# Two service rates of a side-work table in a hybrid attention/recurrence kernel on one core

## The chip, the cores and the metric

The kernel runs on one core of a Trainium2 chip. The metric is the device time of one execution in microseconds (us). The kernel before was timed three times: 4288.13, 4299.74 and 4304.53 us, median 4299.74 us. All rows of profiles below come from a further, profiled execution of 4318.05 us, whose span from the first to the last instruction was 4316.3 us.

## The reference

A latent of 1024 tokens and a context of 256 tokens (width 1024) run through two layers. Cut to what matters here:

```python
for l in range(DEPTH):                                   # DEPTH = 2
    h_lat = rmsnorm(xl, norm1_g[l]) * (1.0 + sc1) + sh1  # h_ctx likewise
    z_lat = jnp.split(h_lat @ w_in[l], IN_SPLITS, axis=-1)
    na_l, na_c = na_mixer(z_lat[0], z_ctx[0], ...)       # 2-D neighbourhood attention
    mla_l, mla_c = mla_mixer(z_lat[1], z_ctx[1], ...)    # latent attention
    rk_l, rk_c = rwkv7_mixer(z_lat[2], z_ctx[2], ...)    # bidirectional RWKV-7 recurrence
    df_l, df_c = diff_mixer(z_lat[3], z_ctx[3], ...)     # differential attention
    xl = xl + g1 * (concat([na_l, mla_l, rk_l, df_l]) @ w_out[l])
    xl = xl + g2 * conv_glu(rmsnorm(xl, ...) * (1.0 + sc2) + sh2, ...)
# the recurrence, both directions, over all tokens:
#   sa = S a_t ;  S = S * w_t + sa b_t^T + v_t k_t^T ;  y_t = S r_t
```

The recurrence is not stepped token by token. It is cut into chunks; inside a chunk the interactions become small triangular matrices, which are inverted once (32x32 blocks first, then joined to 64x64), so that the step over a chunk is a few matrix products.

## The kernel before, in words

**Staging of a layer.** The function `mix` (L1631) does the mixer of one layer in two stages. In the first, the generator `main` runs the input projection: for each group of weight columns, in the order recurrence, values, latent attention ("ml"), differential attention ("diff", written to `dfq` and `dfk`), neighbourhood attention ("na", written to `naq` and `nak`), it loads 512 KB of weights (`wst`), splits them on ACT and DVE into a rounded part `whi` and a rest `wlo` (L1219, L1220), and issues dense matmuls of `whi`, `wlo` on the two parts of the activations (L140, L141, L142, out `psd`), 24 to a chunk of tokens. Rotary work on DVE, ACT and POOL follows (L1332 to L1365) and writes to DRAM. In the second stage an attention loop runs over query blocks: scores `psL` from K and Q (L803), row maxima on DVE (L962, L964), exponentials on ACT (L973), transposes (L1011), products with V (L1032).

**Side work.** Beside both stages run generators that issue a piece of other work each time they are pulled. In the projection stage there are three: `prep_gen` (L283) prepares the recurrence in ten slots, eight or ten steps each (gram products `pg` on PE, L440; masks on DVE, L447 and L448; transposes `pbt`, L460; results to the DRAM buffers `rsg`, `rvt`, `rnt`). `lanes_gen` (L526) inverts the triangular blocks in three groups of slots (0 and 1; 2 to 5; 6 to 9). For each group it loads the blocks (`lM`), does 31 steps of one product and one reduction on DVE (L547, out `lpr`; L548, out `lXT`), copies (L552, `lX`), sends the results to DRAM and back (L554, L557, then L567, L569 and L570 into `G`), and joins blocks with 32x32 matmuls (`pmg`, L580 and L582; 64 of each for group one, 128 for the others). `mla_gen` projects the latent attention's compressed vectors (`mst`, `mpb`, `mpq`, `mpk`, `mpv`); it starts (L1687) once both the ml columns and the ten slots are done. In the attention stage the sides are `scan` (the recurrence proper; it loads `SG`, `VS`, `XB` and waits for the inverse of its slots), `ada` and `rwo`. A group that isn't finished when the projection ends is carried on in the attention stage.

**What sets the order.** `main` yields after every six dense matmuls, the attention loop after each piece of a block. After each yield `tick` pulls every side by its rate from a table:

```python
    s["acc"] += s["rate"]
    while s["acc"] >= 1 and s in self.sides:
        s["acc"] -= 1
        if not self.pull_hi(s["gen"], ...)
```

With rate 0.8 a side issues eight steps in ten ticks. The program order so made is not yet the order of the engines: the kernel is built with a scheduler (L2293) that orders each engine's instructions by this order as priority and by its own estimate of when inputs are ready. Each engine then runs its own list strictly in order, and SP issues almost all DMAs in one list.

Of the kernel before, what the change touches and what calls it, by code (L numbers as in the profile page):

```python
# [40 lines left out]
class K:  # L41
# [1707 lines left out]
    bf3 = (3, 4, 3)  # L1749
    lb2 = ((2, (4, 2, 1)),)  # L1750
    lb3 = ((3, (3, 2, 1)),)
    rates = dict(ada=0.2, prep=0.8, lanes=0.5, scan=0.8, mla=1.5, rwo=0.5)

    def wsp(self, o, n):
        a = max(0, min(n, SEQ - o))
# [545 lines left out]
```

## Time and profile before

| | us |
|---|---|
| median of three runs | 4299.74 |
| profiled execution | 4318.05 |
| its span | 4316.3 |
| PE busy (93% of the span) | 4027.8 |
| DVE busy (66%) | 2866.8 |
| ACT busy (46%) | 1982.7 |
| POOL busy (19%) | 801.9 |

The mean granted clock of TensorE was 0.955 of full speed. Busy time counts an engine's instructions, not what they achieve; a busy PE at half clock counts in full. In the trace the projection stage of the first layer lies between about 110 and 583 us, that of the second between about 2380 and 2846 us; at 583 and at 2846 us the attention stages begin. In the page's 40 slices (108 us each) the granted clock falls to 7 tenths in just two kinds of place besides the start: around these two beginnings.

### The profile page before, as it was taken

To read this page: it belongs to the slowest core of one execution; us is meant where nothing else is said; L and a number is where in the kernel's file an instruction comes from. 1 tells how busy PE (TensorE), PEld (TensorE's weight loads), DVE (VectorE), ACT (ScalarE), POOL (GpSimd) and SP (SyncE) were. 2 spreads that over 40 slices of the span, in tenths; PEclk is the share of its full clock that TensorE was granted. 3 is DMA by queue.
4 is the path that set the end of the run, shared out by engine and by line. 5 is a ranking of instruction groups with operands and counts; after the bars stand their busy time and mean duration, and the time that the engine had idled before them with its cause. 6 is when DMAs were issued, how large, how long until landed. Compare 5 with 4: busy or idle time off the path is not lost. (4 is left out here: it accounts for less than half of the span.)

```text
span 4316.3 us, 76712 instructions
## 1 busy us (share of the span) xinstructions
PE 4027.8 (93%) x29152; PEld 3319.9 (77%) x29152; DVE 2866.8 (66%) x5946; ACT 1982.7 (46%) x4386; POOL 801.9 (19%) x1320
## 2 busy tenths in 40 slices
PE   6999969999999999899998999969999999999998
PEld 4887856677777778788887887856677777788998
DVE  6577686656676765655556667686776766557666
ACT  4444435535554544433334444435545555435443
POOL 3244122212211112000001344122313111111000
PEclk7999979999999999999999999979999999999999
DMA  6444676655523243221213344687636332333332
GB/s 198 151 134 141 204 226 204 224 160 142 151 82 107 78 149 115 71 64 65 64 59 115 137 135 139 204 233 223 206 98 175 104 106 74 125 104 126 94 98 74
DMA packets 423199, 578.40 MB, mean 134 GB/s; under 512 B 109100, under 2 KB 287660, under 8 KB 421296
## 3 DMA queue, kind: packets, MB, share of 16 engines
q1 hardware_dynamic: 422832, 573.51, 42.9%
q8 instruction: 230, 3.77, 0.4%
q14 instruction: 137, 1.12, 0.1%
HBM read 433.47 MB, written 139.92 MB: 133 GB/s over the span
## 5 line engine op out<-in xcount | busy, mean ns | idle before, releaser
L141 PE MATMUL psm<-h_l,whi 128*128 128x512 f32 (+1 forms) x2112 | 710.3, 336 | 9.2 <-DVE h_l L258 9.0
L140 PE MATMUL psm<-h_h,whi 128*128 128x512 f32 (+1 forms) x2112 | 713.5, 338 | 2.3 <-ACT h_h L257 2.3
L142 PE MATMUL psm<-h_h,wlo 128*128 128x512 f32 (+1 forms) x2112 | 709.0, 336 | 0.0
L1888 DVE SCALAR_TENSOR_TENSOR x<-psm,mod,x 128x258 f32<-128x258 f32 (+2 forms) x616 | 327.0, 555 | 288.3 <-PE psm L142 287.9
L973 ACT ACTIVATE sm_P<-psL,sm_n 128x512 f32<-128x512 f32 (+1 forms) x672 | 392.8, 593 | 266.6 <-DVE sm_n L964 238.5
L141 PEld LDWEIGHTS psm<-h_l,whi 128*128 128x128 f32 x2112 | 399.4, 189 | 54.1 <-DVE h_l L258 12.0
L140 PEld LDWEIGHTS psm<-h_h,whi 128*128 128x128 f32 x2112 | 399.4, 189 | 52.0 <-DVE x L1888 4.0
L142 PEld LDWEIGHTS psm<-h_h,wlo 128*128 128x128 f32 x2112 | 399.1, 189 | 43.4 <-issue 0.2
L962 DVE TENSOR_REDUCE sm_m<-psL 128x1 f32<-128x512 f32 (+1 forms) x640 | 353.0, 578 | 88.0 <-PE psL L803 43.3
L140 PE MATMUL psm<-gh,dhi 128*128 128x510 f32 (+3 forms) x1056 | 364.8, 347 | 10.1 <-ACT mb L1852 5.1
L133 ACT ACTIVATE whi<-wst 128x1024 fp32r<-128x1024 f32 x176 | 186.6, 1060 | 401.2 <-PE psm L141 376.7
L141 PE MATMUL psm<-gl,dhi 128*128 128x510 f32 (+3 forms) x1056 | 357.7, 339 | 0.1
L142 PE MATMUL psm<-gh,dlo 128*128 128x510 f32 (+3 forms) x1056 | 357.4, 339 | 0.0
L134 DVE TENSOR_TENSOR wlo<-wst,whi 128x1024 fp32r<-128x1024 f32 x176 | 214.8, 1220 | 169.6 <-ACT whi L133 169.5
L1032 PE MATMUL psV<-PT,V 128*64 128x128 f32 x3488 | 299.3, 283 | 1.2 <-DVE sm_n L964 0.7
L1011 PE MATMUL psT<-ident,sm_P 128*128 128x128 f32 x1744 | 287.3, 287 | 10.6 <-DVE sm_P L1001 6.2
L1032 PEld LDWEIGHTS psV<-PT,V 128*64 128x64 f32 x3488 | 208.8, 137 | 83.7 <-issue 63.7
L1011 PEld LDWEIGHTS psT<-ident,sm_P 128*128 128x128 f32 x1744 | 206.4, 145 | 69.8 <-issue 29.7
L140 PEld LDWEIGHTS psm<-gh,dhi 128*128 128x128 f32 x1056 | 199.6, 189 | 44.6 <-ACT mb L1852 9.3
L142 PEld LDWEIGHTS psm<-gh,dlo 128*128 128x128 f32 x1056 | 200.2, 190 | 21.7
L141 PEld LDWEIGHTS psm<-gl,dhi 128*128 128x128 f32 x1056 | 200.4, 190 | 18.1 <-issue 0.7
L803 PE MATMUL psL<-K,Q 96*128 96x512 f32 (+1 forms) x400 | 148.8, 437 | 68.7 <-DMA Q<-dfq 34.4
(381 smaller groups left out, 9264.7 us busy)
## 6 DMA issues: line engine op xcount, KB each, us to landing
wst<-in_w_up_dram SPq DMA_DIRECT2D x176, 512.0 KB
wst<-in_w_down_dram SPq DMA_DIRECT2D x88, 512.0 KB
adw<-in_ada_w_dram SPq DMA_DIRECT2D x80, 512.0 KB
SG<-rsg SPq DMA_DIRECT2D x40, 896.0 KB
wst<-in_w_out_dram SPq DMA_DIRECT2D x96, 256.0 KB
rsg<-ARM SPq DMA_DIRECT2D x20, 1024.0 KB
K<-dfk SPq DMA_DIRECT2D x16, 960.0 KB
wst<-in_w_rw_dram SPq DMA_DIRECT2D x28, 512.0 KB
```

Source lines behind the costliest of these rows:

```text
L133: nc.scalar.activation(hi[:, :n], st[:, :n], AF.Copy)
L134: nc.vector.tensor_tensor(out=lo[:, :n], in0=st[:, :n], in1=hi[:, :n].bitcast(F32), op=ALU.subtract)
L140: mm(out, ah, bh, start=first, stop=False)
L141: mm(out, ah, bl, start=False, stop=False)
L142: mm(out, al, bh, start=False, stop=last)
L803: nc.tensor.matmul(ps, ld[0][0:96, j], ld[1][j // 2][0:96, j % 2, o:o + n], start=True, stop=True)
L962: nc.vector.tensor_reduce(out=m[:, j, i:i + 1], in_=src, axis=AX.X, op=ALU.max)
L973: ACT(Pt[:, off:off + n], s["L"][j][t][:, to:to + n], AF.Exp, bias=neg, accum_out=sm[:, j, i:i + 1])
L1011: nc.tensor.transpose(pt[:, j], Ph[:, (bb + j) * P:(bb + j + 1) * P], self.ident)
L1032: nc.tensor.matmul(s["po"][64 * h:64 * h + 64, 0], V[:, kts[i], h], s["PT"][h][:, i], start=i == 0, stop=i == nk - 1, tile_position=(0, 64 ...
L1888: STT(out=x[:, s:e], in0=ps[:, s:e], scalar=mod[:, v, 40 + m:41 + m], in1=x[:, s:e], op0=ALU.mult, op1=ALU.add)
```

## The change

One line of numbers (L1752). The preparation is pulled 1.3 times per six dense matmuls where it was 0.8, the inversion 1.2 times where it was 0.5. Nothing else differs; the instructions are the same but for 17 that PE has fewer of, of some 17,900 rows.

```diff
-    rates = dict(ada=0.2, prep=0.8, lanes=0.5, scan=0.8, mla=1.5, rwo=0.5)
+    rates = dict(ada=0.2, prep=1.3, lanes=1.2, scan=0.8, mla=1.5, rwo=0.5)
```

Counted in yields of `main` in the first layer: the ten slots were all issued at yield 180 and are at 134; the second group of the inversion at 222, now 138; the third group's steps began at 224, now 139, and ended at 319, now 178. The projection itself ends at yield 242 in both. The latent attention's side began at 180, now 146. The scheduler then places the instructions. It leaves the first group where it was, and the preparation's slots only three or four chunks earlier in the middle and one chunk at their end.

On PE, at the border between the diff and the na columns of the first layer (`psd` is dense, `pmg` joins inverses of group two, `mst` and `mpb` are the latent attention), before:

```order
L141 MATMUL psd<-H_l_148,whi 128x256
L142 MATMUL psd<-H_h_147,wlo 128x256
L140 MATMUL psd<-H_h_101,whi 128x512
L141 MATMUL psd<-H_l_102,whi 128x512
L142 MATMUL psd<-H_h_101,wlo 128x512
L140 MATMUL psd<-H_h_103,whi 128x512
L141 MATMUL psd<-H_l_104,whi 128x512
L142 MATMUL psd<-H_h_103,wlo 128x512
L580 MATMUL pmg<-G_4899,G_4900 32x32 x4
L1479 MATMUL mpb<-ident,mrs 128x128 x4
L580 MATMUL pmg<-G_4899,G_4900 32x32 x12
L140 MATMUL psd<-H_h_105,whi 128x512
```

and now:

```order
L141 MATMUL psd<-H_l_148,whi 128x256
L142 MATMUL psd<-H_h_147,wlo 128x256
L460 MATMUL pbt<-ident,BK 128x64 x4
L440 MATMUL pg<-ARM,BK 128x128 x4
L580 MATMUL pmg<-G_3986,G_3987 32x32 x16
L440 MATMUL pg<-ARM,BK 128x128 x4
L580 MATMUL pmg<-G_3986,G_3987 32x32 x16
L460 MATMUL pbt<-ident,BK 128x64 x4
L580 MATMUL pmg<-G_3986,G_3987 32x32 x16
L460 MATMUL pbt<-ident,BK 128x64 x4
L1468 MATMUL mst<-sel_74,msq 128x1
L1469 MATMUL mst<-sel_74,msq 128x1
```

Before, the last products `pg` stand at the first matmuls of the na columns, the last `pbt` one and a half chunks of 24 dense matmuls later, and the first `pmg` and `mpb` three chunks later (in the rows above, behind the first chunk of the second na group of weights); the others follow over three chunks more. Now the last `pg` and `pbt`, the first 64 and the next 64 `pmg`, and the first `mst`, `mpb`, `mpq` and `mpk` stand in one clump ahead of the first na matmul. In SP's list the weights of the latent attention (for `mwq`, `mwk` and `mwl`) have moved ahead of all four na weights, where they stood between the second and the third.

On DVE, at the end of the first layer's projection (`lpr` and `lXT` are group three of the inversion, its steps 18 to 20 and 30 to 31; `sm_m` are row maxima of the first attention blocks), before:

```order
L547 TENSOR_TENSOR lpr<-lXT,lM 128x18x18
L962 TENSOR_REDUCE sm_m<-psL 128x1 x4
L548 TENSOR_REDUCE lXT<-lpr 128x18
L964 TENSOR_REDUCE sm_n<-sm_m 128x1
L547 TENSOR_TENSOR lpr<-lXT,lM 128x19x19
L548 TENSOR_REDUCE lXT<-lpr 128x19
L547 TENSOR_TENSOR lpr<-lXT,lM 128x20x20
L962 TENSOR_REDUCE sm_m<-psL 128x1
L548 TENSOR_REDUCE lXT<-lpr 128x20
L962 TENSOR_REDUCE sm_m<-psL 128x1 x2
L547 TENSOR_TENSOR lpr<-lXT,lM 128x21x21
L964 TENSOR_REDUCE sm_n<-sm_m 128x1
```

and now:

```order
L547 TENSOR_TENSOR lpr<-lXT,lM 128x30x30
L891 TENSOR_REDUCE lm<-lt 128x2
L548 TENSOR_REDUCE lXT<-lpr 128x30
L893 TENSOR_TENSOR lm<-lm 128x1
L547 TENSOR_TENSOR lpr<-lXT,lM 128x31x31
L894 TENSOR_SCALAR lm<-lm 128x1
L548 TENSOR_REDUCE lXT<-lpr 128x31
L552 COPY lX<-lXT 64x1024
L962 TENSOR_REDUCE sm_m<-psL 128x1 x4
L964 TENSOR_REDUCE sm_n<-sm_m 128x1
```

Before, steps 18 to 31 of the third group stand between the maxima of the attention's first blocks; now all 31 and the copy `lX` stand ahead of the first of them.

On SP, at the start of the first layer's attention stage (`Q` and `V` are the loads of the attention's blocks, `G` those of group three for joining), before:

```order
L796 DMA K<-dfk 96x2560
L1365 DMA nak<-sp 128x2x256
L799 DMA Q<-dfq 96x4x128
L1444 DMA mlk<-msp 96x2x256
L1444 DMA mlq<-msp 96x2x256 x2
L1444 DMA mlk<-msp 96x2x256
L630 DMA SG<-rsg 128x1792 x4
L799 DMA Q<-dfq 96x4x128
L879 DMA V<-vtm 128x10x128
L799 DMA Q<-dfq 96x4x128
```

and now:

```order
L630 DMA SG<-rsg 128x1792
L631 DMA XB<-rxf 128x256
L1535 DMA adw<-in_ada_w_dram 128x1024 x3
L567 DMA G_4921<-ry_91 32x8x128
L569 DMA G_4921<-rxf 32x8x32 x4
L567 DMA G_4921<-ry_91 32x8x128
L569 DMA G_4921<-rxf 32x8x32 x4
L799 DMA Q<-dfq 96x4x128
L879 DMA V<-vtm 128x10x128
L799 DMA Q<-dfq 96x4x128
```

The twelve loads of `G` and the stores ahead of them have moved in front of the second load of `Q` and the first of `V`; before, they stood far behind these. In the second layer the same moves are found on all three engines.

## Rows read from the trace of the kernel before

**Rows 1.** Windows of the projections' ends and the attention stages' beginnings, columns in its header.

```profile
core 0: us, PE busy (x) PEld busy (x) DVE busy (x) ACT busy (x) POOL busy (x), PEclk, DMA share, GB/s
473.00:583.00 110.00, 108.52 (x882) 95.24 (x882) 71.07 (x150) 58.17 (x108) 14.72 (x17) 1.00 0.69 202
583.00:597.00 14.00, 0.98 (x5) 0.71 (x5) 13.26 (x36) 2.81 (x7) 3.79 (x11) 0.56 0.98 280
597.00:643.00 46.00, 24.66 (x127) 14.62 (x126) 42.27 (x70) 15.14 (x44) 10.66 (x13) 0.50 0.90 274
643.00:690.00 47.00, 36.88 (x491) 26.29 (x488) 31.76 (x72) 23.93 (x71) 16.64 (x32) 0.93 0.70 194
2736.00:2846.00 110.00, 108.88 (x883) 95.33 (x883) 71.28 (x150) 58.14 (x108) 14.29 (x17) 1.00 0.69 202
2846.00:2860.00 14.00, 0.55 (x4) 0.37 (x4) 13.26 (x36) 2.83 (x7) 3.68 (x11) 0.56 0.98 276
2860.00:2902.00 42.00, 21.44 (x97) 12.60 (x97) 38.03 (x65) 14.42 (x43) 6.68 (x8) 0.50 0.96 294
2902.00:2956.00 54.00, 48.70 (x607) 33.36 (x605) 42.49 (x98) 29.34 (x88) 22.92 (x45) 0.97 0.76 217
380.00:473.00 93.00, 82.56 (x442) 68.10 (x443) 80.83 (x135) 36.04 (x83) 42.28 (x44) 0.89 0.44 148
```

**Rows 2.** Windows again, instructions of the inversion's tile `lpr` on DVE alone.

```profile
473.00:583.00 110.00, 1.92 (x11) 1.00 0.69 202
583.00:690.00 107.00, 36.89 (x51) 0.70 0.82 239
2846.00:2956.00 110.00, 37.21 (x51) 0.74 0.86 254
```

**Rows 3.** Timeline of PE at the first attention start: start, duration, instruction, idle before.

```profile
596.35 1.83 PE L803 MATMUL psL<-K,Q 96*128 96x512 f32 x4 [13.02 <-DMA Q<-dfq]
600.69 1.92 PE L803 MATMUL psL<-K,Q 96*128 96x512 f32 x3 [2.52 <-ACT sm_P L973]
605.85 1.92 PE L803 MATMUL psL<-K,Q 96*128 96x512 f32 x3 [3.23 <-ACT sm_P L973]
```

**Rows 4.** Waits from 583 to 690 us: total, times, longest.

```profile
ACT sm_P L973 <- DVE sm_n L964: 24.5, 8, 11.9
PE psL L803 <- ACT sm_P L973: 14.3, 7, 4.0
```

**Rows 5.** Timelines of SP and PE, 590 to 690 us, columns as in rows 3.

```profile
596.80 0.59 SPq L799 DMA_DIRECT2D Q<-dfq  x1
...
672.12 3.86 SPq L569 DMA_DIRECT2D G<-rxf  x5
...
677.49 0.58 SPq L799 DMA_DIRECT2D Q<-dfq  x1
...
683.78 0.76 PE L803 MATMUL psL<-K,Q 96*128 96x512 f32 x1 [7.93 <-DMA Q<-dfq]
```

**Rows 6.** Timelines from the last slot's products to the na weights, four engines.

```profile
473.73 1.71 PE L440 MATMUL pg<-ARM,BK 64*128 64x128 f32 x16
...
484.48 0.40 SPq L489 DMA_DIRECT2D rsg<-ARM  x1
...
489.32 0.85 ACT L1219 ACTIVATE mwq<-wst 128x768 fp32r<-128x768 f32 x1 [3.09 <-DMA rsg<-ARM]
...
495.57 1.06 ACT L1219 ACTIVATE whi<-wst 128x1024 fp32r<-128x1024 f32 x1 [2.15 <-DMA wst<-in_w_na_dram]
...
496.66 1.23 DVE L1220 TENSOR_TENSOR wlo<-wst,whi 128x1024 fp32r<-128x1024 f32 x1 [2.79 <-ACT whi L1219]
```

**Rows 7.** Groups of instructions on PE from 473 to 583 us: busy, mean ns.

```profile
L140 PE MATMUL mpq<-mh,mwq 128*96 128x256 f32 x40 | 11.7, 292 | 0.0
L580 PE MATMUL pmg<-G,G 32*32 32x32 f32 x128 | 6.0, 193 | 0.0
```

**Rows 8.** The product L547 alone, group two in the projection and group three behind it.

```profile
340.00:456.00 116.00, 24.11 (x31) 0.93 0.50 162
570.00:650.00 80.00, 23.26 (x31) 0.64 0.83 245
```

**Rows 9.** Timelines of DVE and POOL from 639 us.

```profile
639.07 2.87 DVE L998 SCALAR_TENSOR_TENSOR rt<-sm_t,lm,rr 128x1 f32<-128x1 f32 x1
...
639.43 2.48 POOL L852 TENSOR_TENSOR nb<-nb,msk 128x512 f32<-128x512 f32 x2
```

## The prediction

> **What bounds the kernel now.** I read the slices first: the granted clock falls to 7 tenths at two beginnings, those of the attention stages. The windows then show what is lost there. The last 110 us of the first projection are PE's: PE is busy 108.52 of 110, DVE 71.07. In the next 14 us PE does nothing, then in 46 us it is busy 24.66 at a granted clock of 0.50, the lower of its two levels (1.2 GHz), while DVE is busy 42.27 [rows 1]. So PE bounds the projection, and DVE bounds the first 60 us of attention. The second layer repeats it: 108.88 of 110, then 0.55 of 14, then 21.44 of 42 at 0.50 with DVE at 38.03 [rows 1].
>
> What fills DVE there is the inversion: of the 38.8 us of its third group 36.89 lie behind 583 us in the first layer, 37.21 behind 2846 us in the second [rows 2]. PE's timeline gives the rhythm: a score group of 1.8 to 1.9 us every 5 us or so, with 2.52 and 3.23 us idle between [rows 3]. The list of waits names the loop: the exponential waited 24.5 us for the row maxima's result on DVE, and PE 14.3 us for the exponentials that free the score banks [rows 4]. The maxima stand between inversion steps in DVE's list, so each maximum pays for a step. A second stall is SP's: loads of G issued just before delay a load of Q to 677.49 us, and PE idles 7.93 us for it [rows 5].
>
> **The gain at the attention start.** The change puts all 31 steps and the copy ahead of the first maximum. First layer: PE idles 107 − (0.98 + 24.66 + 36.88) = 44.5 us between 583 and 690 [rows 1]; 13.0 of that is the load of K and Q [rows 3], which stays. Of the other 31.5 I keep three fillings of the score pipeline at 2.5 us [rows 3], 7.5, since the maxima and exponentials of the first blocks still precede any other work: 24 gained. Half of the 12.3 us that 24.66 us at half clock cost comes back if idling is shorter: +6. Against it, the second Q and first V, issued at 596.80 and after, now stand behind twelve G loads; five took 3.86 us of SP [rows 5], so twelve take 9.3, about half of it covered by the first block's four score groups: −5. Sum 25. Second layer: 110 − (0.55 + 21.44 + 48.70) = 39.3, less 13.5 for the load (14 us with 0.55 busy) and 7.5, is 18.3; clock +5, SP −4: 19 to 20, taken as 20. Bounds: at the best every microsecond behind the load is work at full clock, 107 − (0.98/2 + 24.66/2 + 36.88) − 13 = 44 and 110 − (0.55/2 + 21.44/2 + 48.70) − 13.5 = 37. At the least only the SP stall of 7.9 goes in the first layer, and nothing in the second, because other DVE work takes its place.
>
> **The cost in the projection.** The steps don't vanish. The last 110 us then hold 71.07 + 36.89 = 108 us of DVE work [rows 1, 2]. Elsewhere DVE reaches 80.83/93 = 87% where the preparation runs and 42.27/46 = 92% where the inversion's steps fill it [rows 1]; the steps have few waits, so I take the second: 108/0.92 = 117.4, a stage 7.4 us longer; at 87% it is 124, 14 longer. PE's cover, which hid DVE before with 39 us to spare, is gone.
>
> To this comes the clump at the diff/na border. Before, dense na matmuls ran while the last slot's chain went its way: from the products at 473.73 over the store of ARM at 484.48 and mwq at 489.32 to the na weights' rounded part at 495.57 and rest at 496.66, ending at 497.89 [rows 6], 24.2 us. Those weights were for a later group then. Now the uq and ukv weights go ahead of the first na weights, so PE has only the clump's own work under this chain: gram products 1.7 [rows 6], 128 joining matmuls 6.0, one batch of `mpq`, which is 11.7/10 = 1.2 for each of three parts, so 3.5 [rows 7], and I estimate 4 for the rest by their likeness to these. That is 15.2 of 24.2, 9.0 us idle; if no other DMAs delay the chain, 5.5. A stall costs half clock behind it besides, as at 597 us [rows 1], a few microseconds. But DVE may do inversion steps in this stall, so stall and DVE time overlap. I take 10 for the stage: 7.4 and a third of the 9. Bounds: −4, if slots that start three to four chunks earlier relieve the stretch from 380 to 473 us, where PE idles 10.4 [rows 1], and nothing is added behind; +34, the slow rival below. The second layer has the same rows, so another 10. The other moved pieces (first group in place, its loads, the earlier slots) cost nothing: they lie beside PE work that is longer than theirs, and nothing behind them waits; their cover gone is the −4 with its sign turned.
>
> A rule that speaks against the move concerns DVE and POOL. Row: a DVE operation on 128x1, `rt` at 639.07, took 2.87 us and ended at 641.94, when two POOL products that began at 639.43 (1.24 us each) ended at 641.91 [rows 9]. The Trainium skill (SBUF — State Buffer, Who interferes with whom) says that a DVE instruction with two SBUF inputs and a GpSimd instruction that reads SBUF exclude each other for the whole instruction. L547 has two SBUF inputs, so by the rule all of POOL's time in the stage could be added. But L547's 31 products took 24.11 us inside the projection and 23.26 behind it [rows 8], 0.85 more, and by rows that is its price; it is in the rounding above.
>
> **Sum.** Gains 25 + 20, costs 10 + 10: −25 on the profiled execution, 4318.05 to 4293. That execution stands 18.3 us (0.4%) over the median of the runs; the difference is carried over: 4299.74 − 25 = 4275 us.
>
> **Rivals.** B, slower: the na stage becomes DVE's own, with waits inside. DVE runs its list in order, and the latent attention's pieces (PE sum, DVE scale, PE, ACT, DVE) now stand between inversion steps (1.25 us on the mean, 38.8/31), so DVE waits for PE and PE for DVE. At 80% of 135 us the stage is 25 longer, plus the stall of 9, 34. The copy `lX` comes late and the G round trip with it, so the gain is 12 a layer: +22 each, 4344 us. It decides where DVE's share stays below 110 + 10 + 12 = 132, that is 82%. For it: DVE had 87% in its busiest projection stretch, with lists of just this kind. Against: steps of the inversion depend on nothing but DVE itself.
>
> C, no change: the gain goes into SP's list. If the twelve G loads wait for the copy's stores to land, the second Q and V wait with them, as the third Q did for 7.93 us [rows 5]; the score pipeline then starves for some 12 us more, the gain is 13 and 8, and the cost 10 each: 4299 us. For it: the twelve stand in front now. That the change does less than it says belongs here, since the scheduler left the first group in place and the slots' end but one chunk earlier.
>
> D, much faster: PE goes on binding the projection, since the steps fill DVE's gaps (39 us free); cost 2 a layer, gains 40 and 35: 4299.74 − 71 = 4229 us. Against: 108 of 110 leaves no slack for one wait.
>
> E: POOL blocks the steps in full. POOL is busy 14.72 and 14.29 us in the two stages [rows 1]; the stage grows by that besides 10: −45 + 20 + 29 = +4, 4304 us. This is what the Trainium skill's rule (SBUF — State Buffer, Who interferes with whom) would do at worst; rows 8 speak against it.
>
> **Chances.** Forecast 0.45, between 4260 and 4290; C 0.20; B 0.18; D 0.13; E 0.04. About 0.5%, 21.5 us, is what a measurement of this kernel can tell from no change, so faster means below 4278, slower above 4321. Of the forecast's 0.45, 0.27 lie below 4278; with D and a little of C that is 0.42 faster. Same: 0.18 of the forecast, C's and E's rest, 0.38. Slower: B and a little of E and C, 0.20. The range is 4230 to 4325: it takes in C, E, the forecast and most of D, and leaves out most of B.
>
> **What would show it.** In the changed kernel's profile: tile `lpr` with nearly no DVE time in attention; score groups 2.5 to 3 us apart at the start where they were 5; a shorter stretch at 0.50 clock behind the K and Q load. The cost: a PE gap of 5 to 9 us before the first na matmul, and a stage from the last gram products to the last projection matmul of about 120 us with DVE at 90% or more. DVE at 82% or less there, with PE waiting for `mz` or `mh`, would be B. A PE wait for the second Q of over 10 us would be C. No PE gap and a stage of 110 would be D. The forecast is wrong in its sum if the start of attention stays at 5 us a group without inversion steps in it: then DVE wasn't what bound it.

## The result and the profile after

The changed kernel is slower: 4348.13 us (median of four runs, 4340.77 to 4352.89) against 4299.22 us, a ratio of 1.0116, 95% interval 1.0089 to 1.0142. The forecast was 4275 us. Its profiled execution took 4352.16 us, span 4350.4, 34.1 over the span of before. (The profiled execution of before took 18.8 us more than the median of its timed runs, that of the changed kernel 4.0 more than its own, so lags against the trace of before read 14.8 us low in all; where in the trace those lie is not known.)

I counted matmuls to find where the time went. The pages of both kernels list the same number of instructions on every engine (29152 records of matmuls on PE, not 17 fewer), so the n-th dense matmul, score matmul (`psL`) or output matmul (`pso`) of a layer, n counted from 0, is the same work in both traces. The difference of their ends is the lag there, in us:

```
                               before    lag of after, layer 1   layer 2
last diff group (dense 1008)    449.5                    +4.8     +25.0
its last matmul (dense 1079)    473.6                    -2.0     +18.3
first na matmul (dense 1080)    473.8                   +30.3     +47.7
in that na group (dense 1120)   485.9                   +39.0     +50.8
last dense matmul               580.9                   +18.5     +38.7
first score matmul              597.1                   +22.6     +44.0
score matmul 60                 698.7                   +15.6     +38.9
score matmul 480               1065.6                    +5.4     +30.0
first output matmul            1148.4                   +19.7     +32.6
end of the span                4316.3                             +34.1
```

(The times are those of the first layer; the second's projection stage starts with a lag of 20.7.) So each layer loses 14 us net between the start of the last diff group and the last dense matmul: some 30 at the border to the na columns and more in the first of them, less 7 that are won just before it and some 20 that come back behind it, where the clump's work no longer stands between dense matmuls. It loses 4 to 5 more up to the first scores. It wins 17 and 14 in the attention, and the first layer loses 14 again at the attention's end.

The windows of after that answer to [rows 1], same columns, the first five from the first layer and the last from the second:

```profile
473.00:503.00 30.00, 27.83 (x297) 26.11 (x297) 12.22 (x23) 17.00 (x33) 1.61 (x2) 0.55 0.77 249
503.00:532.00 29.00, 27.55 (x191) 24.41 (x192) 16.93 (x47) 11.26 (x21) 6.84 (x7) 0.93 0.68 179
532.00:592.00 60.00, 57.76 (x343) 49.33 (x342) 58.15 (x115) 27.75 (x53) 5.95 (x7) 1.00 0.46 143
592.00:619.00 27.00, 6.42 (x53) 6.13 (x51) 23.51 (x31) 6.20 (x13) 7.05 (x11) 0.70 0.81 228
619.00:665.00 46.00, 31.32 (x293) 22.66 (x293) 17.56 (x42) 17.75 (x50) 1.48 (x4) 0.57 0.93 244
2755.00:2785.00 30.00, 27.13 (x274) 24.94 (x275) 15.00 (x27) 17.74 (x35) 1.61 (x2) 0.60 0.81 263
```

The first row is the clump. PE is busy there almost throughout, but at a clock of 0.55, where [rows 1] have 1.00 for the whole stretch. I summed such windows, 3 us each, from dense matmul 1000 to the last: idle PE time, time lost by a clock under 1 (busy time by 1 minus the clock), and work at full clock. Before: 4.3 idle, 2.9 slow, 125.2 work. After: 8.7 idle, 15.0 slow, 123.0 work; in the second layer 5.0, 2.9, 125.4 against 10.6, 14.4, 122.6. By this count 12 of the 14 us lie in busy time at half clock. That is where the time lies, not what full clock would give back, as the chain below shows.

The inversion on DVE, as in [rows 2]:

```profile
473.00:512.00 39.00, 0.00 (x0) 0.61 0.70 218
512.00:592.00 80.00, 23.07 (x50) 1.00 0.54 160
592.00:619.00 27.00, 16.18 (x13) 0.70 0.81 228
619.00:700.00 81.00, 0.00 (x0) 0.64 0.77 217
```

No step runs in the clump, though DVE is idle for 18 of its 30 us: the third group's blocks are stored by the last slot and its tiles are in use by the second group's joins. From 512 us on its steps run beside the rotary work and the latent attention's pieces (23.07 us of `lpr` up to 592), DVE is full (58.15 of 60 us from 532), and no step is left in the attention.

The chain of [rows 6] in after, timelines of ACT, DVE and PE:

```profile
473.37 1.13 PE L440 MATMUL pg<-ARM,BK 64*128 64x128 f32 x8 [0.82 <-ACT BT L464]
490.14 0.84 ACT L1219 ACTIVATE mwq<-wst 128x768 fp32r<-128x768 f32 x1 [1.00 <-DMA rsg<-ARM]
496.22 1.04 ACT L1219 ACTIVATE whi<-wst 128x1024 fp32r<-128x1024 f32 x1
497.29 1.23 DVE L1220 TENSOR_TENSOR wlo<-wst,whi 128x1024 fp32r<-128x1024 f32 x1 [1.87 <-ACT whi L1219]
503.29 0.77 PE L140 MATMUL psd<-H_h,whi 128*128 128x512 f32 x1
```

The last gram products began at 473.37 and 476.92, so the na weights were ready (498.5) some 25 us behind, as the prediction read from before. PE came to them only at 503.29, since its clump ran at half clock. The hole is the one that was foreseen; it is full of slow work and not empty. At full clock PE would have reached the na matmuls 4.8 us earlier (6.0 if the rounded part alone lets it start), and would have idled before them.

PE at the attention's start, as in [rows 3]:

```profile
618.94 1.83 PE L803 MATMUL psL<-K,Q 96*128 96x512 f32 x4 [19.59 <-DMA Q<-dfq]
622.89 1.92 PE L803 MATMUL psL<-K,Q 96*128 96x512 f32 x3 [2.12 <-ACT sm_P L973]
625.85 1.92 PE L803 MATMUL psL<-K,Q 96*128 96x512 f32 x3 [1.04 <-ACT sm_P L973]
629.43 1.25 PE L803 MATMUL psL<-K,Q 96*128 96x512 f32 x2 [1.66 <-ACT sm_P L973]
...
641.77 1.08 PE L1556 MATMUL adaps<-adw,sc 128*32 128x256 f32 x8 [8.86 <-DMA adw<-in_ada_w_dram]
```

The score groups do come closer, 3.0 to 3.9 us apart where they were 4.3 to 5.2. But the wait for K and Q is 19.6 us and not 13.0, and then PE, in order, waits 8.9 us for a modulation weight. DVE and SP tell why:

```profile
607.44 0.41 DVE L1364 TENSOR_TENSOR sp<-zt,sp 128x256 fp32r<-128x256 f32 x1
```

```profile
606.60 0.85 SPq L796 DMA_DIRECT2D K<-dfk  x2
607.88 0.38 SPq L1365 DMA_DIRECT2D nak<-sp  x1
608.31 0.75 SPq L799 DMA_DIRECT2D Q<-dfq  x1
...
635.69 1.54 SPq L1535 DMA_DIRECT2D adw<-in_ada_w_dram  x3
...
642.93 4.60 SPq L569 DMA_DIRECT2D G<-rxf  x4
647.58 0.59 SPq L799 DMA_DIRECT2D Q<-dfq  x1
```

The first Q stands behind the last store of `sp`, and DVE's last `sp` stood between inversion steps until 607.85, 8.5 us after the last dense matmul. The adw loads stand behind the stores of `lXT` and `lX`, and the second Q is issued at 647.58, 39 us after the first. Before, it was issued at 596.80 [rows 5], 9.8 us after the first:

```profile
587.03 0.64 SPq L799 DMA_DIRECT2D Q<-dfq  x1
```

At the first layer's attention end (PE, then SP):

```profile
1161.43 1.41 PE L803 MATMUL psL<-K,Q 96*128 96x512 f32 x3 [7.18 <-DMA Q<-dfq]
1167.30 0.79 PE L140 MATMUL pso<-h_h,wohi 128*128 128x512 f32 x1 [4.46 <-ACT h_h L1776]
```

```profile
1130.54 1.40 SPq L2035 DMA_DIRECT2D x<-in_xT_dram  x3
1142.69 0.33 SPq L784 DMA_DIRECT2D ymix<-oy  x1
...
1148.81 1.98 SPq L799 DMA_DIRECT2D Q<-dfq  x2
```

SP stood from 1131.94 to 1142.69 at the last store of the recurrence's output, and behind it waited the loads of the last blocks.

### The profile page after: what moved, and what is told of

Read it like the earlier page. It is cut to its first block, busy times and chain, and to the rows that moved or that the text cites. A ratio compares the mean times of both kernels' runs of the same rounds, so it can differ in the third digit from the quotient of the medians.

```text
span 4350.4 us, 76716 instructions
## 1 busy us (share of the span) xinstructions
PE 4057.6 (93%) x29152; PEld 3353.1 (77%) x29152; DVE 2881.3 (66%) x5946; ACT 1983.3 (46%) x4386; POOL 809.0 (19%) x1320
## 4 chain that ended last, share of the span: by engine, by line
PE 67%; DVE 7%; DMA 6%; SPq 2%; issue 2%; ACT 2%; POOL 1%; DVEq 0%; POOLq 0%; ACTq 0%
PE psm L140 12%; PE psm L141 12%; PE psm L142 12%; PE psV L1032 6%; PE psT L1011 5%; PE psL L803 2%; PE pso L140 1%; PE pso L142 1%; PE pso L141 1%; PE psL L873 1%; PE psd L140 1%; PE psL L140 1%; PE psd L141 1%; PE psd L142 1%; PE adaps L1556 1%
```

## Experiments

Ratios are to the kernel before on the same chip, with 95% intervals; lags are against the trace of before, first layer then second, the second's with its start subtracted. The edits are shown by their main lines.

**1. The latent attention held back**, everything else as changed:

```diff
-            if F["prep"] and F.get("ml"):
+            if F["prep"] and F.get("ml") and F["n"] >= 180 + 28 * l and not F.get("mla"):
```

> The changed kernel, with the latent attention's side held back until yield 180 of the projection (208 in the second layer), as late as before; all 31 steps of the third group stay ahead of the attention. Its order has no clump at the border to the na columns: dense matmuls stand between the pg, pmg, mst and mpb. Clump theory (28 us at half clock at the border, some 15 us lost a layer, and SP's list costs the rest): 30 us faster than the changed kernel from the clump and some 15 more because the second Q now stands ahead of the G loads, so 4300 to 4320. DVE theory (the 37 us of steps make the na stage DVE's own, whatever stands at its border): 4345, as the changed kernel.

Measured 4324.77, ratio 1.0043 (1.0023 to 1.0064). The clump's stretch in its windows, and the start of attention:

```profile
473.00:503.00 30.00, 30.00 (x284) 25.83 (x283) 14.86 (x27) 14.98 (x30) 2.09 (x2) 0.89 0.82 278
600.00:633.00 33.00, 2.66 (x10) 1.55 (x9) 23.22 (x25) 2.67 (x5) 8.57 (x13) 0.50 0.85 248
```

```profile
602.01 1.44 PE L803 MATMUL psL<-K,Q 96*128 96x512 f32 x3 [0.90 <-ACT mt L1506]
632.89 1.32 PE L580 MATMUL pmg<-G,G 32*32 32x32 f32 x21 [29.44 <-DMA G<-ry]
```

```profile
621.45 0.67 DVE L962 TENSOR_REDUCE sm_m<-psL 128x1 f32<-128x512 f32 x1
```

The lag of the last dense matmul is +3.3 and −3.6, where it was +18.5 and +18.0: with the clump goes most of the projection's loss (some 4 us of it is PE work that has moved behind the stage). But now the first scores come at 600.5 us, where they came at 618.9, and DVE isn't done: the first maximum comes at 621.45, behind the last step, and PE stands 29.4 us in front of the joins, whose loads follow the copy of the last step. The 60th score lags 16.9. The expectation had the first half right and missed the second.

**2 and 3. One rate alone.** `lanes=1.2` with `prep=0.8`, and `prep=1.3` with `lanes=0.5`.

> Only lanes=1.2, prep stays 0.8. All 31 steps of the third group ahead of the attention, pieces of the border spread over four chunks, second Q ahead of the G loads on SP. Clump theory: no stretch at 0.5 clock at the border, 4295 to 4315. DVE theory: the same DVE work in the same stage, 4340 to 4350.

> Only prep=1.3, lanes stays 0.5. The border has its clump of pg, pmg, mst, mpb and mpq (64 pmg instead of 112), 27 of 31 steps stand ahead of the attention, the second Q stands ahead of the G loads. Clump theory: a stretch of some 25 us at 0.5 clock at the border, 12 us a layer, against some 10 gained at the start of attention: 4300 to 4315. DVE theory: 27 of 31 steps cost nearly what 31 do, 4335 to 4345.

Measured 4331.18 (1.0058; 1.0032 to 1.0085) and 4330.56 (1.0054; 1.0031 to 1.0076), each 16 us over the upper end of what the clump theory gave. The inversion's rate alone leaves the dense work on time (+0.1), but the first scores come 19 us late in both layers: ahead of them in PE's list stand the latent attention's last products, which wait for ACT, and ACT for DVE and for a DMA.

```profile
614.24 0.58 PE L140 MATMUL mpv<-mwk,mh 128*128 128x256 f32 x1 [15.27 <-ACT mt L1495]
```

The preparation's alone has a clump with some 64 joins (11.1 us lost by the clock), of which most comes back, because those pieces are missing later; the last dense matmul is 6.7 late. So neither rate is harmless, and neither costs the whole.

**4. The round trip held** until yield 290, ahead of the stores at L554:

```diff
+            while s0 == 6 and F["n"] < 290 + 28 * l:
+                yield
```

> The changed kernel, with the third group's stores, loads and joins held back until yield 290 (318 in the second layer), in the attention stage; clump and DVE steps as in the changed kernel. SP theory (in the first 60 us of attention PE waits for adw and the second Q behind those DMAs): the 8.9 us gap before the first adaps goes and the second Q issues within 10 us of the first; 10 a layer gained, 4325 to 4335. Rival (the wait goes to the next transfer in the list, or to DVE): 4340 to 4355.

Measured 4325.77, 1.0043 (1.0025 to 1.0060).

```profile
615.98 1.83 PE L805 MATMUL psL<-K,Q 96*128 96x512 f32 x4 [19.68 <-DMA Q<-dfq]
618.61 0.78 PE L666 MATMUL pall<-VS,SG 128*64 128x64 f32 x8 [0.80 <-DMA SG<-rsg]
619.93 1.92 PE L805 MATMUL psL<-K,Q 96*128 96x512 f32 x3 [0.54 <-ACT sm_P L975]
622.00 0.70 PE L666 MATMUL pall<-VS,SG 128*64 128x64 f32 x8 [0.16 <-DMA SG<-rsg]
622.89 1.92 PE L805 MATMUL psL<-K,Q 96*128 96x512 f32 x3 [0.19 <-ACT sm_P L975]
```

The 8.9 us gap is gone from here and the score groups stand 3 to 4 us apart. Between the first and the 480th score the first layer gains 28.9 (17.2 in the changed kernel). In the second layer it gains 5.0 where the changed kernel gains 14.0: PE waits elsewhere for adw. The clump stays (projection +15.4 and +15.6).

**5. Both holds.**

> The changed kernel with both holds: the latent attention's side until yield 180, the third group's stores, loads and joins until yield 290 (28 more in the second layer). No clump at the border, and PE's list has the joins behind the first score groups. If the two losses add (the border's, 14 to 18 us a layer at the projection's end, and the round trip's, some 20 at the attention's start), the end of the projection stands where it does before the change, and the first layer's attention gains 20 to 29, the second's 5 to 15: 4260 to 4290, faster than both. If another wait takes their place (SP's list is as long as ever): 4305 to 4325.

Measured 4337.31, 1.0075 (1.0054 to 1.0095): worse than either, and over both of the ranges. The dense work ends earlier than before (−3.4 and −6.0), and then PE idles 31 us in both layers. The first maximum stands behind the late steps:

```profile
618.08 2.20 DVE L964 TENSOR_REDUCE sm_m<-psL 128x1 f32<-128x512 f32 x4
```

PE's wait ends at 630.69 with a load of `VS` that stands in SP's list behind the third group's stores. The losses don't add; I read it so that the clump's delay had been covering the steps.

**6. One wide matmul for 16 small joins** of the second group.

> The changed kernel, with the 16 small joining matmuls of each batch of the second group replaced by one 32x32x512 matmul (the joined blocks of slots 2 to 5 are then not the inverse's). Chain theory (the first na matmul waits for its weights, which come 25 us after the last gram products whatever PE does): PE idles where the joins stood, and the lag of the first na columns, 34 us with the joins, falls by at most 5. Clock theory (28 us of small matmuls at half clock are the border's length): it falls by some 12, the joins' time at half clock.

One run, 4342.48. It doesn't tell the theories apart: the wide matmul takes as long as the 16 (each of these matmuls makes two records). The changed kernel's batch, then this run's:

```profile
478.92 1.91 PE L580 MATMUL pmg<-G,G 32*32 32x32 f32 x32
473.38 1.91 PE L580 MATMUL pmg<-G,G 32*32 32x512 f32 x2 [0.86 <-DMA G<-ry]
```

**7 and 8. The third group's steps left out**, of the kernel before and of the changed one:

```diff
-            for t in range(1, 32):
+            for t in range(1, 32 if s0 < 6 else 1):
```

> The kernel before, without the 31 steps of the third group (slots 6 to 9 are then not inverted); their copy, stores, loads and joins stay. If the row maxima behind those steps are what bound the first 60 us of attention, as the prediction had it, the score groups start 2.5 to 3 us apart, and the first layer gains 20 to 30 by its 60th score group. If SP's loads or the joins bind it: under 10.

> The changed kernel, without the 31 steps of the third group (slots 6 to 9 are then not inverted); the clump stays. DVE theory (DVE's 97% busy in the last 60 us of the projection is its bound): the projection ends 8 to 15 us earlier in each layer, and the wait for K and Q falls from 19.6 to 13. If DVE only just keeps up: the projection's end moves by under 3, and only the wait for K and Q shrinks, by 5 to 7.

One run each, 4290.22 and 4287.78. In the kernel before, the joins moved ahead of the first scores and PE waited for them, but from the first score to the 60th 22 us are gained in the first layer and 15 in the second, to the 480th 40 and 20. The groups start 3.5 to 4.0 us apart, and PE's waits for the exponentials there, 2.5 and 3.2 us before, fall to 0.6 at most: the maxima behind the steps were a bound there. But the first score itself comes 14 us later behind the last dense matmul than before. Counted from that matmul, only 7.8 and 1.4 us are gained up to the 60th score, 25.8 and 6.3 up to the 480th, and on the clock 13 us in all (4290.22 against 4303.36). In the changed kernel the projection doesn't get shorter without the steps (from the 1000th dense matmul to the last 154.7, with the third group's joins in it, 16.2 of it lost by the clock); the clump is as it was:

```profile
472.00:502.00 30.00, 28.16 (x304) 26.13 (x304) 14.25 (x26) 16.75 (x32) 2.94 (x3) 0.56 0.77 248
```

Only the wait for K and Q shrinks, to 15.5 us. So DVE at 97% did not bound the dense matmuls; it bound what comes right behind them.

Without these steps the two kernels take the same time, though the clump is still in the second: its last dense matmul lags 24.6 us in the first layer, its 60th score 0.9. So by these two runs the changed kernel's loss of 49 us needs the steps; the clump alone is made good behind the projection.

**9. A staging tile of its own** for the uq weights:

```diff
-                    t = K.wp.tile([P, 1024], F32, tag="wst", name="wst")
+                    t = s.stage(s.i) if s.stage else None
+                    if t is None:
+                        t = K.wp.tile([P, 1024], F32, tag="wst", name="wst")
```

> The changed kernel; only the staging tile of the latent attention's uq weights is its own (3 KB a partition) where it was one of the two that the dense weights go through. Chain theory (the clump stands because both staging tiles are held by uq and ukv until the last slot's ARM and NT are stored, so the first na weights come 25 us late): the order has no clump any more, and the lag of the first na columns (34 us with it) falls to under 5, though both rates stay; the steps then run late, and PE waits some 30 us behind the first score groups as with the held side; 4320 to 4335 in all. Rival (the rates themselves crowd the border): the lag stays over 20.

```profile
470.00:500.00 30.00, 26.27 (x244) 22.06 (x243) 16.00 (x28) 17.03 (x36) 0.00 (x0) 0.88 0.85 267
```

With both rates kept, the order has no clump, the clock is 0.88 where it was 0.55, and what is lost from the start of the last diff group into the first na group (dense 1008 to 1120) falls from 34.2 to 2.5 us in the first layer, from 25.8 to 6.1 in the second. So the clump came from the two staging tiles that uq and ukv hold. In the second layer, where about as much PE work lies in the stage as in the changed kernel, dense 1000 to the last takes 132.7 us, where it took 147.6, and 133.3 before the change. The time is 4352.13, ratio 1.0102 (1.0080 to 1.0124), worse than the 4320 to 4335 expected: in the first layer PE waits 8.5 and 7.7 us for ACT's `mt` ahead of and among the first scores, and then for the joins' loads behind the last step; in the second the wait for Q is 17.0 us, where it was 13.5.

```profile
639.97 1.88 PE L580 MATMUL pmg<-G,G 32*32 32x32 f32 x32 [22.84 <-DMA G<-rxf]
```

**10 to 12. The steps of group three before the joins of group two**, to start them earlier: with the changed rates and the held side, with the changed rates and the staging tile, and with the old rates.

> The changed rates, latent attention held until yield 180, and the inversion in another order: the steps of group three before the joins of group two (they share their tiles), both joins from yield 270 on. If the third group's late start is what puts its steps on the attention's path (it waits for group two's joins until some 525 us): its steps start some 35 us earlier, beside dense work, they end before the first maximum is due, the 30 us gap of the held version goes, and 20 a layer are gained over the kernel before: 4255 to 4275. If DVE has no idle time to give there, or SP's list takes over: 4295 to 4325.

> The kernel before with its old rates, only the order of the inversion changed: steps of group three before the joins of group two. If the late start alone decides, the old rates do as well, since the steps start at some 485 us either way: 4255 to 4280. If the rates are needed to have the steps issued early enough: 4290 to 4305.

Measured 4396.51 (1.0198; 1.0176 to 1.0220), 4401.33 (1.0214; 1.0191 to 1.0237) and 4368.09 (1.0137; 1.0118 to 1.0156); the second was expected at 4255 to 4280 as well, or over 4295 if the latent attention's pieces crowd DVE. Only this last held; the first and third are slower than either of their ranges. The steps now end at 577 to 578 us, but work of the latent attention stands behind them on DVE, and its PE work is pushed past the dense matmuls, where PE waits for it (old rates):

```profile
593.40 0.53 PE L140 MATMUL mpq<-mh,mwq 128*96 128x256 f32 x1 [14.05 <-ACT mt L1501]
...
608.84 0.58 PE L140 MATMUL mpv<-mwk,mh 128*128 128x256 f32 x1 [11.27 <-ACT mt L1501]
```

This is close to the slow rival's mechanism, as is run 2: late pieces of the latent attention, and PE waiting for them, though here ACT in turn waits 13.6 us for a DMA (`mlk`). It exists; it wasn't what the changed kernel's projection showed.

**13. The recurrence's output stored by ACT's queue**, not SP's.

> The changed kernel; only the store of the recurrence's output (ymix from oy) is issued by ACT where SP issued it. Theory (in the first layer SP stood 12 us at the last of these stores, behind it waited the loads for the last attention blocks, and PE waited 7.2 and 4.5 us): between the 480th score group and the first output matmul the lag no longer grows by 14 us but by 0 to 3; in all some 14 us less, 4330 to 4338. Rival (the recurrence's output itself is late and holds the output projection): the 14 us stay.

Measured 4352.76, 1.0115 (1.0095 to 1.0135). In the profile the first layer's lag at the attention's end grows by 9.9 and not 14.3, and PE's wait for Q is 1.9 and not 7.2; its wait for h_h (4.5) stays. So SP's blocked store was a third of that loss, and on the clock nothing remains of it.

**14 to 17. Versions meant to beat both**: the round trip held until yield 340 at the old rates; prep alone with the hold at 290; that with the staging tile; that with the held side (expected as the one with the tile: 4280 to 4290, or 4300 to 4315).

> The kernel before with its old rates; the third group's stores, loads and joins held until yield 340. The third Q now stands ahead of the G loads on SP. If the 7.9 us PE gap at 676 us is SP's alone: it goes, 4 to 8 us in the first layer, 0 to 5 in the second, 4290 to 4298. If the next load in the list takes over: 4300 to 4310.

> prep=1.3 alone with the round trip held until yield 290. With prep alone the projection's end was only 3 us late, in spite of a clump, and the attention's start had gained 22 in the first layer. If holding the round trip gives as much here as in the changed kernel (8 to 12 a layer): 4295 to 4310, level with the kernel before. If the lag comes from elsewhere (the wait for K and Q, 19 us here): 4320 to 4335.

> prep=1.3 alone, the round trip held until yield 290 and the own staging tile for uq: all harms that were found are taken away at once. The order has no clump, 24 of 31 steps stand ahead of the first maximum and the rest between the maxima as before. If the found terms are the whole loss (clump 11 us of half clock a layer in the run with prep alone and the hold, attention's start already at its gain): 20 us faster than that run, 4280 to 4290, faster than before. If DVE's work only moves about (no clump, but a later first maximum, as with the staging tile in the changed kernel): 4300 to 4315.

Measured: 4308.47 (1.0004; 0.9992 to 1.0016), 4304.97 (0.9997; 0.9985 to 1.0008), 4335.54 (1.0060; 1.0040 to 1.0081), over both of its ranges, and 4314.72 (1.0014; 0.9999 to 1.0029). None beats the kernel before. With the clump taken out of the second, its projection is no shorter (134.8 and 137.9 against 134.8 and 138.7 us): the slow time is halved, and work that had been done in the clump comes back as work later. That the three terms are the whole loss is refuted.

## Why the prediction was wrong

**The projection's cost** was taken as 10 us a layer; it is 17.8 and 19.0 up to the first score (13.7 + 4.1 and 13.7 + 5.3). The step that failed here is "DVE may do inversion steps in this stall, so stall and DVE time overlap", by which only a third of the 9 us stall was counted. No step ran in the stall, since group three's blocks weren't there yet (no `lpr` from 473 to 512). And half clock was named without a figure, "a few microseconds", and behind the stall, where the stretch itself ran at it. The chain of 24 us was right (25). Priced at the spacing that the same instructions have at full clock in the trace of before, the clump's work is some 17 us (an estimate; the prediction's 15.2 took the 128 records of L580 in [rows 7] for all the joins, though L582 has 5.9 us more). That leaves a stall of 8, near the 9.0; then the slow clump ran 4.8 over the chain. Counted in full, these two are most of the 13.7. That the clump makes the projection's loss is shown by run 9, in its second layer, and by run 1, which remove it by different means. It is not the kernel's whole loss: run 9 has no clump and takes 4352 us; run 15 has one and is level with the kernel before; run 8 has one and, without the steps, is level with run 7, which has none.

**DVE's 7.4 us** in that stage were wrong as a cost of dense work: without the steps (run 8) the projection is no shorter. The steps' price is paid behind the projection, as 4 to 5 us more of the wait for K and Q, or, where the clump is gone, as 23 to 31 us for which PE stands behind the first scores (runs 1, 5 and 9): the first maxima come only behind the last step, and the loads that end the wait stand behind that step's copy.

**The gain of 25 + 20** came out as 17.2 + 14.0 from the first to the 480th score. Its mechanism was right as far as the groups closed up; but even with the steps left out altogether (run 7, where PE waits for the joins instead) only 13 us are gained on the clock, so 45 for moving them was too much. What was mis-sized in the sum is SP, −5 and −4 in the sum: the second Q came 30 us later and a wait for adw of 8.9 us took its place. Run 4, without that queue, gains 28.9 in the first layer. That it gains 5.0 in the second stays open; PE waits 7.6 and 4.1 us for adw there.

**What had no term**: 14.3 us at the first layer's attention end (2.6 in the second), where the recurrence's output ran late and blocked SP, a third of it by run 13; and 3.7 and 4.3 us before the last diff group, where the preparation's slots moved and I had put zero. "They lie beside PE work that is longer than theirs, and nothing behind them waits" is the second step that failed. With the start and the end (3.6) these add up to the profile: 17.8 + 19.0 − 31.2 + 16.9 + 8.0 + 3.6 = 34.1. From the forecast's −25 that is 59.1 us: 16.8 in the projection, 13.8 in the gain, and 28.5, the largest share, where the sum had no term. The 14.8 us by which the trace of before was slow come on top and are not placed.

**The rivals.** B's 4344 is nearest to the time, but its mechanism, DVE and PE waiting for each other at a DVE share of 82% or less, is not what happened: DVE's share was lower still (94 of 126 us from 473 to 599), but because it idled beside the clump, while PE was busy 119 of the 126. That B came near is luck. The forecast's own signs of its cost, a PE gap of 5 to 9 us and DVE at 90% in a stage of 120, did not show either. C named a mechanism that is there (SP's list, worth about 12 us in the first layer) with too small a cost beside it. E is refuted in its size: the third group's steps took 39.2 us on DVE, 38.8 before.

What stays open: the second layer's attention in run 4, the rest of the loss at the attention's end (it is 3.3 us in run 4's trace and 4.1 in run 6's, whose round trip stands as in the changed kernel, so it isn't tied to one cause here), and where the 7 to 11 us before the last diff group come from in the later versions with prep at 1.3.

## What to carry to other kernels

A faster service rate for side work moves its waits too, and above all what it holds: look in the order for places where the main work's staging tiles are taken by side work that can't yet use them, and price the whole stretch. Here PE ran at half clock in it from end to end, and reached the dense matmuls 4.8 us after their weights were ready. Work that is taken off one in-order list's path is charged to whatever stands behind it next (DVE's steps to the first maximum, the round trip to the next Q), so removing the visible loss alone gave little here, and two repairs did not add. A version without the side work at all (runs 7 and 8) gives a first measure of what its place can be worth.

## What was not expected of the hardware

TensorE stayed at the lower of its two levels, 1.2 GHz, while it was busy nearly all the time with small matmuls. In the changed kernel's windows:

```profile
484.00:488.00 4.00, 4.00 (x39) 3.98 (x39) 1.28 (x3) 1.47 (x4) 0.98 (x1) 0.50 1.02 383
496.00:500.00 4.00, 4.00 (x43) 3.66 (x42) 1.23 (x1) 2.00 (x4) 0.00 (x0) 0.50 0.41 92
```

It had fallen at 476 us, behind gaps of 0.5 to 1.1 us between the last slot's pieces, and rose at 507 us, when PE had gone back to dense matmuls at 503:

```profile
504.00:508.00 4.00, 4.00 (x35) 3.55 (x34) 1.96 (x3) 0.00 (x0) 2.83 (x2) 0.63 0.68 197
508.00:512.00 4.00, 4.00 (x42) 3.69 (x40) 1.31 (x4) 3.09 (x7) 0.00 (x0) 1.00 0.37 59
```

Between dense matmuls the same joins left it at 1.00 [rows 1]. And 16 joins of 32x32 or one of 32x512 took the same 1.91 us there (run 6). The joins lost less than half of their speed by it: four batches took 6.0 us at 1.00 [rows 7], 1.5 each.
